# A hybrid decoder layer on one core: the last attention pair ahead of two gate blocks, weight differences at a fixed place, results picked up one unit later

## The chip, the cores and the metric

The kernel runs on one core of a Trainium2 chip. The metric is device time in microseconds for one call. TensorE (PE) multiplies matrices, VectorE (DVE) and ScalarE (ACT) do the elementwise work, GpSimd (POOL) issues some transfers, and SyncE (SP) issues the weight loads. Each engine works through its own instructions in order.

## The reference

Input x is 256 tokens of 2048 channels, all in float32. A pre-norm is followed by one wide input projection and two token mixers: a gated delta rule over 8 heads (short convolution, decays, a triangular inverse in chunks of 64), and causal attention over 8 heads of 128. With 256 tokens there is one attention block, so no past block is ever chosen. Both results are gated, widened to 2048 channels, merged and projected once more:

```python
proj = h @ w_in                      # q, k, v, z of both mixers, gate_a, gate_b
u_a = oa @ w_branch_a                # 256 x 1024 by 1024 x 2048
u_b = (ob * silu(moba_z)) @ w_branch_b
merged = sigmoid(gate_a) * u_a + sigmoid(gate_b) * u_b
x = x + rms_norm(merged @ w_out, post_norm_w)
```

## The kernel before, in words

**Split weights.** Every weight tile is loaded in float32 by SP (`raw`, 1 MB, three buffers) and split into a rounded half `hi`, cast by ACT (L218), and a rest `lo`, subtracted by DVE (L219), each with three buffers. A product is then three matmuls (hi by hi, lo by hi, hi by lo) into PSUM, which has 4 `acc` banks for projections and 4 `aux` banks for all smaller work. One split of 128 x 1024 elements feeds 12 matmuls of 512 columns in a gate block, or 16 mixed ones in a query or key block. That is one **unit** of the kernel's clockwork below.

**Blocks and ORDER.** The string `ORDER` (L42) is the sequence of blocks on PE. `q`, `kq`, `v` are the delta rule's projections, `zg` and `zm` the two output gates, `mv` attention's values, and `mk0` to `mk3` attention's queries and keys of two heads each. `ga0` to `ga3` and `gb0` to `gb3` are blocks of 512 columns of the two merging gates (`sigmoid_gate`, L708). `ua0` and `ua1` are pairs of 512-column blocks of `oa @ w_branch_a`. After ORDER come the four blocks of branch b (`branch`, L1036, "ub"), with their merging, and the output projection (`y`).

**Seven products for a pair.** A pair (`seven`, L766) is a 2 x 2 block product done with seven products in place of eight. It needs sums of quarters of the activations (`oas`, made by `turned_outputs`, L913) and differences of quarters of the weights (`tq`, three tiles fetched by POOL at L724 and subtracted by DVE in six operations at L731). Between its products it takes `fill` work: the four row blocks of one gate, before the change ga2 for the first pair and ga3 for the second. `done` (L804) multiplies a finished quarter, c11, c12, c22 or c21, into the gate. The first pair's differences are asked for inside `solve`; `next_differences` (L818) asks for those of the second pair and then for those of the output projection.

**Queues.** Everything that isn't a projection stands in queues of Python generators. While a projection is written down, `tick()` (L136) runs after every half unit and lets each queue go on when its wait is over. A generator says with `yield n` how many units it waits. `gq` holds the delta rule (`decays`, `score_pair`, `inverse`, `solve`), `vq` its values, `aq` two queues of attention heads (`attend`, L979), `bq` the turning of attended heads, `mq` the merging, and `sq` the differences (`differences`, L726, which first waits T_WAIT). So a wait in units says beside which projection work an instruction is written down. While `turned_outputs` runs, `held` stops `aq` and `bq`, because it keeps all four `aux` banks.

**attend** writes the scores after A_WAIT1 = 1.5 units, the transposes of the softmaxed scores A_WAIT2 later, and the product with the values A_WAIT3 later. Its two heads run side by side in two queues.

**What fixes the order on an engine.** The order of writing is a wish: an instruction whose inputs are expected early can be moved ahead of earlier ones on its engine. `pin` holds an instruction behind the one written just before it on the same engine. All PE work is pinned. Of DVE's work a part is, not the differences at L731.

Of the kernel before, what the change touches and what calls it, by code (L numbers as in the profile page):

```python
# [8 lines left out]
F32 = mybir.dt.float32  # L9
F32R = mybir.dt.float32r  # L10
BF16 = mybir.dt.bfloat16
AF = mybir.ActivationFunctionType
ALU = mybir.AluOpType
AX = mybir.AxisListType

P = 128
# [11 lines left out]
LC_WAIT = (1.5, 1.5, 1.5, 3.5)  # L28
INV = (0.6, 2)
SLOW = 8  # L30
T_WAIT = 3
V_WAIT = 8
SV_WAIT = 1
OS_WAIT = 3
A_WAIT1 = 1.5
A_WAIT2 = 6
A_WAIT3 = 3
A_WAIT4 = 4

ORDER = (  # L42
    "q0 mv0 zg0 q1 kq2 kq3 zg1 v0 v1 v2 ga0 zm0 zm1 mv1 v3 mk0 mk1 mk2 ga1 mk3 ua0 gb0 gb1 ua1 gb2 gb3"
).split()


# [28 lines left out]
def hybrid_layer(  # L75
# [15 lines left out]
    nc = tc.nc  # L91
    B, S, D = x.shape
    NT = S // P
    KT = D // P
    H = a_log.shape[1]
# [6 lines left out]
    w_in = w_in.rearrange("o d f -> (o d) f")  # L102
# [6 lines left out]
    CGA = CMQ + 4 * GW  # L109
    CGB = CGA + D  # L110

    cst = ctx.enter_context(tc.tile_pool(name="cst", bufs=1))
    big = ctx.enter_context(tc.tile_pool(name="big", bufs=1))
    wraw = ctx.enter_context(tc.tile_pool(name="wraw", bufs=3))
    wspl = ctx.enter_context(tc.tile_pool(name="wspl", bufs=3))
    wk = ctx.enter_context(tc.tile_pool(name="wk", bufs=2))
# [7 lines left out]
    def aux_tile(name):  # L124
        return aux.tile([P, 512], F32, tag="aux", name=name)
# [6 lines left out]
    extra = []  # L132
# [418 lines left out]
    def lazily(make):  # L551
        made = []

        def get():
            if not made:
                made.append(make())
            return made[0]

        return get
# [125 lines left out]
        v_left[0] -= 1  # L685
        after[0] = SLOW

    ga012 = big.tile([P, D // 512 - 1, NT, 512], F32, tag="ga", name="ga")

    ga3 = lazily(lambda: big.tile([P, NT, 512], F32, tag="ga3", name="ga_3"))  # L690

    def ga(c, t):
        return ga012[:, c, t, :] if c < 3 else ga3()[:, t, :]


    def free_tile(shape, dtype, tag, name):
        gq.drain()
# [5 lines left out]
    def ob_tile():  # L703
        while not obs:
            gq.tick()
        return obs[0]

    def sigmoid_gate(n, col, c):  # L708
        pts = proj_n(w_in, col + c * 512, hT, KT, f"{n}{c}")
        for t in range(NT):  # L710
            tl = ga(c, t) if n == "ga" else gb_tile()[:, c, t, :]
            nc.scalar.activation(tl, pts[t], AF.Sigmoid, scale=rstd[:, t : t + 1])

    oaT = [None]

# [10 lines left out]
    def differences(tq, c, wait):  # L726
        yield wait
        for o, a, b in ((0, 0, 2), (1, 1, 0), (2, 1, 2)):
            for u in range(2):
                us = slice(2 * u, 2 * u + 2)  # L730
                nc.vector.tensor_tensor(tq[o][:, us], tq[a][:, us], tq[b][:, us], op=ALU.subtract)  # L731
                yield 1
        formed.append(c)

# [27 lines left out]
    def load(w, h, c, name):  # L762
        raw = wraw.tile([P, 4, 512], F32, tag="raw", name=f"raw_{name}{c}_{h}")
        nc.sync.dma_start(raw, w[h * 512 : (h + 1) * 512, c * 512 : (c + 1) * 512].rearrange("(k p) c -> p k c", p=P))
        return raw

    def seven(quarter, s_, tq, w, c, banks, name, fill=lambda i: None, done=lambda b: None):
        c11, c12, c21, c22 = banks
        s5 = tq[0][:, 0]
        product([quarter(0, 0)], load(w, 0, c, name), [c21], [True], f"{name}p1")  # L770
        fill(0)
        product([s_[0]], tq[0], [c12], [True], f"{name}p5")
        nc.scalar.copy(c11, c21)
        product([s_[1]], tq[1], [c21], [False], f"{name}p6")
        nc.scalar.copy(s5, c12)
        fill(1)
        raw21 = load(w, 1, c, name)
        nc.vector.tensor_tensor(c12, c21, s5, op=ALU.add)
        product([quarter(0, 1)], raw21, [c11], [False], f"{name}p2")
        for u in range(2):  # L780
            us = slice(2 * u, 2 * u + 2)
            nc.vector.tensor_tensor(tq[1][:, us], raw21[:, us], tq[1][:, us], op=ALU.subtract)  # L782
        product([s_[2]], tq[2], [c21], [False], f"{name}p7")
        fill(2)
        nc.vector.tensor_tensor(c22, c21, s5, op=ALU.add)
        done(c11)
        product([s_[3]], load(w, 1, c + 1, name), [c12], [False], f"{name}p3")
        fill(3)
        done(c12)
        done(c22)  # L790
        product([quarter(1, 1)], tq[1], [c21], [False], f"{name}p4")
        done(c21)

    def branch_pair(i):
        c = 2 * i
        while not oas or c not in formed:
            sq.tick()
            gq.tick()
        c11, c12, c21, c22 = (acc_tile(f"a_ua{c}_{n}") for n in ("11", "12", "21", "22"))
        place = {id(c11): (c, 0), id(c12): (c + 1, 0), id(c21): (c, 1), id(c22): (c + 1, 1)}  # L800

        def done(b):
            cc, t = place[id(b)]
            nc.vector.tensor_tensor(ga(cc, t), ga(cc, t), b, op=ALU.mult)  # L804


        quarter = quarters(hT)
        pts = [aux_tile(f"a_ga{2 + i}_{t}") for t in range(NT)]

        def gate(h):  # L810
            raw = load(w_in[:, CGA : CGA + D], h, 2 + i, "ga")
            product([quarter(0, h), quarter(1, h)], raw, pts, [h == 0] * 2, f"ga{2 + i}_{h}")
            if h == 3:
                for t in range(NT):
                    nc.scalar.activation(ga(2 + i, t), pts[t], AF.Sigmoid, scale=rstd[:, t : t + 1])

        seven(quarters(oaT[0]), oas, tqs[-1], wa, c, (c11, c12, c21, c22), f"ua{c}", fill=gate, done=done)

    def next_differences(w, c):

        for q in aq + bq:
            q.drain()
        tqs.append([big.tile([P, 4, 512], F32, tag=f"z{i}", name=f"tq{len(tqs)}_{i}") for i in range(3)])
        for i in (0, 2, 1):
            fetch(tqs[-1], w, c, i)
        formed.clear()
        sq.add(differences(tqs[-1], c, T_WAIT))

    def solve():
# [83 lines left out]
        def turned_outputs(ozs):  # L913


            a = {}
            for t in (1, 0):
                for g in range(2):
                    pt = aux_tile(f"ot_{t}_{g}")
                    for hh in range(4):  # L920
                        tr(pt[:, hh * P : (hh + 1) * P], ozs[t][:, g, hh, :], ident)
                    a[t, g] = pt.rearrange("p (h n) -> p h n", n=P)
                for g in range(2):
                    ks = slice(4 * g, 4 * g + 4)
                    halved(oT[:, ks, t * P : (t + 1) * P], oT[:, ks, S + t * P : S + (t + 1) * P], a[t, g])
                yield 1
            oa_f = big.tile([P, 2, 4, P], F32, tag="tv", name="oa_f")
            x, y = (oa_f[:, i] for i in range(2))
            nc.scalar.copy(x, a[1, 1])
            nc.vector.tensor_tensor(a[1, 1], a[1, 0], x, op=ALU.add)  # L930
            nc.scalar.copy(y, a[0, 0])
            nc.vector.tensor_tensor(a[0, 0], a[1, 1], y, op=ALU.subtract)
            nc.scalar.copy(x, a[0, 0])
            yield 0.5
            nc.vector.tensor_tensor(a[0, 1], a[0, 1], x, op=ALU.subtract)
            nc.vector.tensor_tensor(a[1, 0], y, a[1, 0], op=ALU.subtract)
            yield 0.5
            sums = [None] * 4
            for i, o, tag in ((0, (1, 1), "tt"), (1, (0, 0), "tw"), (3, (0, 1), "ga3"), (2, (1, 0), "tv")):
                tl = big.tile([P, 2, 4, P], F32R, tag=tag, name=f"oas_{i}")  # L940
                sums[i] = tl[:, 0], tl[:, 1]
                halved(*sums[i], a[o])
                yield 0.5
            oas.extend(sums)
# [19 lines left out]
            fetch(tqs[0], wa, 0, i)  # L964
        sq.add(differences(tqs[0], 0, T_WAIT))
        yield OS_WAIT
        held.append(True)
        yield from turned_outputs(ozs)
        held.pop()
# [3 lines left out]
    def attention_values(c):  # L973
        pts = proj_n(w_in, CMV + c * 512, hT, KT, f"mv{c}")
        for t in range(NT):
            nc.scalar.activation(mv[:, t, c * 512 : (c + 1) * 512], pts[t], AF.Copy, scale=rstd[:, t : t + 1])


    def attend(h, qT, kT):  # L979
        yield A_WAIT1  # L980
# [16 lines left out]
            tr(pp[:, b * P : (b + 1) * P], s[:, b * P : (b + 1) * P], ident)  # L997
        pT = wk.tile([P, 3 * P], F32, tag="pT", name=f"pT_{h}")
        nc.scalar.copy(pT, pp[:, : 3 * P])
        yield A_WAIT3  # L1000
        po = aux_tile(f"po_{h}")
        hc = slice(h * P, (h + 1) * P)
# [31 lines left out]

    def branch(c):
        pb = proj_n(wb, c * 512, ob_tile(), H, f"ub{c}")  # L1036
        for t in range(NT):
            nc.vector.tensor_tensor(gb_tile()[:, c, t, :], gb_tile()[:, c, t, :], pb[t], op=ALU.mult)  # L1038
        for t in range(NT):
            nc.vector.tensor_tensor(ga(c, t), ga(c, t), gb_tile()[:, c, t, :], op=ALU.add)  # L1040

    for m in range(4):
        kTs[m // 2].append(halves(pfirst[m], f"k{m}"))
# [65 lines left out]

    for c in range(D // 512):  # L1110
        branch(c)
        mq.add(merge(c, 0.5 if c < 3 else 5))


    quarter = quarters(mT)
# [54 lines left out]
    c = 3  # L1170
    pts = [acc_tile(f"a_y{c}_{t}") for t in range(NT)]
    keep = []
    for tg, n in (("g0", 4), ("ga", 3), ("ga3", 1), ("u1", 4)):
        tl = big.tile([P, n, 2, 512], F32R, tag=tg, name=f"keep_{tg}")
        keep += [tl[:, i] for i in range(n)]
    parts = []
# [53 lines left out]
```

## Time and profile before

| | |
|---|---|
| median of 3 runs | 792.16 us (789.65 to 792.6) |
| profiled execution | 790.07 us, span 788.4 us |
| mean granted clock of TensorE | 0.994 |
| matmuls | 3923 |
| memory read, written | 149.61 MB, 3.15 MB |

A row of a timeline gives the start and the duration in us, the engine, the line, what is written from what, the count of merged instructions, and in brackets the idle time of the engine before it and what ended that. A row of the windows gives for a stretch the busy time and count of each engine, then the granted clock as a share of full speed, the busy share of the DMA engines and GB/s. The profile's names leave out buffer numbers: `a_mq` is the PSUM bank of an attention query projection, `a_ga` of a gate block, `tq` a tile of weight quarters. In the trace mk2 lies at 363 to 402.5 us, ga1 at 402.5 to 434.5, mk3 at 434.5 to 465.4, the first pair at 465.4 to 513.7, gb0 and gb1 at 513.7 to 559.2, the second pair at 559.2 to 602.6, gb2 and gb3 at 602.6 to 646.5, branch b at 646.5 to 694.3, and the output projection after it.

### The profile page before, as it was taken

To read this page: it belongs to the slowest core of one execution; us is meant where nothing else is said; L and a number is where in the kernel's file an instruction comes from. 1 tells how busy PE (TensorE), PEld (TensorE's weight loads), DVE (VectorE), ACT (ScalarE), POOL (GpSimd) and SP (SyncE) were. 2 spreads that over 40 slices of the span, in tenths; PEclk is the share of its full clock that TensorE was granted. 3 is DMA by queue.
4 is the path that set the end of the run, shared out by engine and by line. 5 is a ranking of instruction groups with operands and counts; after the bars stand their busy time and mean duration, and the time that the engine had idled before them with its cause. 6 is when DMAs were issued, how large, how long until landed. Compare 5 with 4: busy or idle time off the path is not lost. (4 is left out here: it accounts for less than half of the span.)

```text
span 788.4 us, 10325 instructions
## 1 busy us (share of the span) xinstructions
PE 767.4 (97%) x3923; PEld 651.6 (83%) x3923; DVE 565.0 (72%) x914; ACT 425.3 (54%) x642; POOL 29.0 (4%) x53
## 2 busy tenths in 40 slices
PE   8999999999999999999999899999999999999996
PEld 7998988898888888888888688878877888787884
DVE  5777679886768898774556968784588546878573
ACT  5676665656544444454454756634554444556551
POOL 3000000102000000011001000100000000000000
PEclk9999999999999999999999899999999999999999
DMA  8485766459864656659337362766467564584542
GB/s 306 162 259 187 206 187 170 141 178 227 263 209 163 211 170 205 183 165 241 101 114 266 105 204 83 280 234 203 173 224 270 200 211 163 163 315 170 208 158 106
DMA packets 93399, 153.42 MB, mean 195 GB/s; under 512 B 3109, under 2 KB 46758, under 8 KB 92710
## 3 DMA queue, kind: packets, MB, share of 16 engines
q1 hardware_dynamic: 88902, 134.42, 52.7%
q0 software_dynamic: 3872, 17.31, 6.9%
q10 hardware_dynamic: 576, 1.05, 0.4%
q8 instruction: 30, 0.49, 0.3%
q14 instruction: 19, 0.16, 0.1%
HBM read 149.61 MB, written 3.15 MB: 194 GB/s over the span
## 5 line engine op out<-in xcount | busy, mean ns | idle before, releaser
L144 PE MATMUL a_ga<-hi_ga,hT 128*128 128x512 f32 x256 | 84.1, 396 | 0.0
L144 PE MATMUL a_gb<-hi_gb,hT 128*128 128x512 f32 x256 | 79.2, 389 | 0.0
L219 DVE TENSOR_TENSOR lo_gb<-raw_gb,hi_gb 128x1024 fp32r<-128x1024 f32 x32 | 38.9, 1222 | 26.6 <-ACT hi_gb L218 26.6
L144 PEld LDWEIGHTS a_gb<-hi_gb,hT 128*128 128x128 f32 x256 | 48.1, 188 | 9.9
L144 PEld LDWEIGHTS a_ga<-hi_ga,hT 128*128 128x128 f32 x256 | 48.1, 188 | 9.6
L218 ACT CAST hi_gb<-raw_gb 128x1024 fp32r<-128x1024 f32 x32 | 33.4, 1053 | 41.3 <-PE a_gb L144 37.5
L219 DVE TENSOR_TENSOR lo_ga<-raw_ga,hi_ga 128x1024 fp32r<-128x1024 f32 x32 | 38.8, 1222 | 23.5 <-ACT hi_ga L218 23.3
L144 PE MATMUL a_ga<-lo_ga,hT 128*128 128x512 f32 x128 | 50.4, 394 | 2.2 <-DVE lo_ga L219 2.2
L144 PE MATMUL a_gb<-lo_gb,hT 128*128 128x512 f32 x128 | 50.1, 391 | 1.7 <-DVE lo_gb L219 1.7
L144 PE MATMUL a_mq<-hT,hi_mq 128*128 128x512 f32 x128 | 48.7, 419 | 2.8 <-ACT hi_mq L218 2.8
L218 ACT CAST hi_ga<-raw_ga 128x1024 fp32r<-128x1024 f32 x32 | 33.4, 1052 | 25.6 <-PE a_ga L144 13.5
L144 PE MATMUL a_zg<-hi_zg,hT 128*128 128x348 f32 (+1 forms) x192 | 47.0, 322 | 0.0
L144 PE MATMUL a_mk<-hT,hi_mk 128*128 128x512 f32 x128 | 46.4, 404 | 0.0
L144 PE MATMUL a_y<-hi_y,mT 128*128 128x512 f32 x144 | 45.9, 391 | 0.0
L144 PE MATMUL a_q<-hT,hi_q 128*128 128x512 f32 x128 | 45.8, 398 | 0.0
L144 PE MATMUL a_v<-hT,hi_v 128*128 128x512 f32 x128 | 45.5, 399 | 0.1
L144 PE MATMUL a_ub<-hi_ub,obT 128*128 128x512 f32 x128 | 41.2, 394 | 0.0
L144 PE MATMUL a_k<-hT,hi_k 128*128 128x512 f32 x128 | 40.4, 398 | 0.5 <-ACT hi_k L271 0.5
L144 PE MATMUL a_zm<-hi_zm,hT 128*128 128x512 f32 x128 | 40.6, 392 | 0.0
L144 PE MATMUL a_mv<-hi_mv,hT 128*128 128x512 f32 x128 | 40.1, 390 | 0.0
L144 PE MATMUL a_mq<-hT,lo_mq 128*128 128x256 f32 x128 | 37.1, 290 | 1.1 <-DVE lo_mq L219 1.1
L144 PE MATMUL a_v<-hT,lo_v 128*128 128x256 f32 x128 | 36.0, 282 | 0.8 <-DVE lo_v L219 0.8
(362 smaller groups left out, 1958.6 us busy)
## 6 DMA issues: line engine op xcount, KB each, us to landing
raw_ga<-in_w_in_dram SPq DMA_DIRECT2D x16, 1024.0 KB, 5.2
raw_gb<-in_w_in_dram SPq DMA_DIRECT2D x16, 1024.0 KB, 5.1
raw_y<-in_w_out_dram SPq DMA_DIRECT2D x15, 1024.0 KB, 5.0
raw_q<-in_w_in_dram SPq DMA_DIRECT2D x8, 1024.0 KB, 5.6
raw_mv<-in_w_in_dram SPq DMA_DIRECT2D x8, 1024.0 KB, 5.1
raw_v<-in_w_in_dram SPq DMA_DIRECT2D x8, 1024.0 KB, 5.7
raw_zm<-in_w_in_dram SPq DMA_DIRECT2D x8, 1024.0 KB, 5.3
raw_mq<-in_w_in_dram SPq DMA_DIRECT2D x8, 1024.0 KB, 5.7
```

Source lines behind the costliest of these rows:

```text
L144: return pin(nc.tensor.matmul(*args, **kwargs))
L218: nc.scalar.copy(hi, raw)
L219: nc.vector.tensor_tensor(lo, raw, hi.bitcast(F32), op=ALU.subtract)
```

## The change

Six edits, with no change to what is computed:

1. ORDER: mk3 follows mk2 directly; ga1 and ga2 are blocks ahead of the first pair; ga3 is the first pair's filling and gb2 the second's.
2. Waits: A_WAIT2 6 to 4, A_WAIT3 3 to 2, T_WAIT 3 to 7, and the first three merges wait 1.5 units where they waited 0.5.
3. The differences at L731 are pinned, and `next_differences` asks for its three tiles in another order.
4. `turned_outputs` waits until all eight heads have their softmax transposed; the sums for the product p3 lie in two softmax buffers ("s") in place of a tile of their own.
5. The gate of branch a is one tile of four blocks in place of three and one.
6. c21's multiplication, and branch b's multiplications and additions, go into a new queue `dq` and are written down one unit later.

```diff
-T_WAIT = 3
+T_WAIT = 7
...
-A_WAIT2 = 6
-A_WAIT3 = 3
+A_WAIT2 = 4
+A_WAIT3 = 2
...
-    "q0 mv0 zg0 q1 kq2 kq3 zg1 v0 v1 v2 ga0 zm0 zm1 mv1 v3 mk0 mk1 mk2 ga1 mk3 ua0 gb0 gb1 ua1 gb2 gb3"
+    "q0 mv0 zg0 q1 kq2 kq3 zg1 v0 v1 v2 ga0 zm0 zm1 mv1 v3 mk0 mk1 mk2 mk3 ga1 ga2 ua0 gb0 gb1 ua1 gb3"
...
-    ga012 = big.tile([P, D // 512 - 1, NT, 512], F32, tag="ga", name="ga")
-    ga3 = lazily(lambda: big.tile([P, NT, 512], F32, tag="ga3", name="ga_3"))
+    ga_ = big.tile([P, D // 512, NT, 512], F32, tag="ga", name="ga")
...
-                nc.vector.tensor_tensor(tq[o][:, us], tq[a][:, us], tq[b][:, us], op=ALU.subtract)
+                pin(nc.vector.tensor_tensor(tq[o][:, us], tq[a][:, us], tq[b][:, us], op=ALU.subtract))
...
-        done(c21)
+        dq.add(later(lambda: done(c21)))
+
+    dq = Queue()
+    extra.append(dq)
+
+    def later(f):
+        yield 1
+        f()
...
+        n, g, col = (("ga", 3, CGA), ("gb", 2, CGB))[i]
+        pts = [aux_tile(f"a_{n}{g}_{t}") for t in range(NT)]
...
-        for i in (0, 2, 1):
+        for i in (2, 0, 1) if len(tqs) == 2 else (1, 0, 2):
             fetch(tqs[-1], w, c, i)
...
+                    sums[i] = [wk.tile([P, 4, P], F32R, tag="s", name=f"oas_{i}_{n}") for n in ("hi", "lo")]
...
         yield OS_WAIT
+        while attended[0] < H:
+            yield 0.5
         held.append(True)
         yield from turned_outputs(ozs)
...
+        attended[0] += 1
         yield A_WAIT3
...
+        def weighted():
+            for t in range(NT):
+                nc.vector.tensor_tensor(gb_tile()[:, c, t, :], gb_tile()[:, c, t, :], pb[t], op=ALU.mult)
+            for t in range(NT):
+                nc.vector.tensor_tensor(ga(c, t), ga(c, t), gb_tile()[:, c, t, :], op=ALU.add)
+
+        dq.add(later(weighted))
...
-        mq.add(merge(c, 0.5 if c < 3 else 5))
+        mq.add(merge(c, 1.5 if c < 3 else 5))
...
-    for tg, n in (("g0", 4), ("ga", 3), ("ga3", 1), ("u1", 4)):
+    for tg, n in (("g0", 4), ("ga", 4), ("u1", 4)):
```

More of the change, by code (lines that the diff above doesn't have):

```diff
@@ L686, in values @@
         after[0] = SLOW
-    ga012 = big.tile([P, D // 512 - 1, NT, 512], F32, tag="ga", name="ga")
-    ga3 = lazily(lambda: big.tile([P, NT, 512], F32, tag="ga3", name="ga_3"))
+    ga_ = big.tile([P, D // 512, NT, 512], F32, tag="ga", name="ga")
     def ga(c, t):
-        return ga012[:, c, t, :] if c < 3 else ga3()[:, t, :]
+        return ga_[:, c, t, :]
     def free_tile(shape, dtype, tag, name):
@@ L706, in ob_tile, with gate_place @@
         return obs[0]
+    def gate_place(n, c, t):
+        return ga(c, t) if n == "ga" else gb_tile()[:, c, t, :]
     def sigmoid_gate(n, col, c):
@@ L710, in sigmoid_gate @@
         for t in range(NT):
-            tl = ga(c, t) if n == "ga" else gb_tile()[:, c, t, :]
-            nc.scalar.activation(tl, pts[t], AF.Sigmoid, scale=rstd[:, t : t + 1])
+            nc.scalar.activation(gate_place(n, c, t), pts[t], AF.Sigmoid, scale=rstd[:, t : t + 1])
     oaT = [None]
@@ L807, in branch_pair @@
         quarter = quarters(hT)
-        pts = [aux_tile(f"a_ga{2 + i}_{t}") for t in range(NT)]
+        n, g, col = (("ga", 3, CGA), ("gb", 2, CGB))[i]
+        pts = [aux_tile(f"a_{n}{g}_{t}") for t in range(NT)]
         def gate(h):
-            raw = load(w_in[:, CGA : CGA + D], h, 2 + i, "ga")
-            product([quarter(0, h), quarter(1, h)], raw, pts, [h == 0] * 2, f"ga{2 + i}_{h}")
+            raw = load(w_in[:, col : col + D], h, g, n)
+            product([quarter(0, h), quarter(1, h)], raw, pts, [h == 0] * 2, f"{n}{g}_{h}")
             if h == 3:
                 for t in range(NT):
-                    nc.scalar.activation(ga(2 + i, t), pts[t], AF.Sigmoid, scale=rstd[:, t : t + 1])
+                    nc.scalar.activation(gate_place(n, g, t), pts[t], AF.Sigmoid, scale=rstd[:, t : t + 1])
         seven(quarters(oaT[0]), oas, tqs[-1], wa, c, (c11, c12, c21, c22), f"ua{c}", fill=gate, done=done)
@@ L938, in turned_outputs @@
             sums = [None] * 4
-            for i, o, tag in ((0, (1, 1), "tt"), (1, (0, 0), "tw"), (3, (0, 1), "ga3"), (2, (1, 0), "tv")):
-                tl = big.tile([P, 2, 4, P], F32R, tag=tag, name=f"oas_{i}")
-                sums[i] = tl[:, 0], tl[:, 1]
+            for i, o, tag in ((0, (1, 1), "tt"), (1, (0, 0), "tw"), (3, (0, 1), None), (2, (1, 0), "tv")):
+                if tag:
+                    tl = big.tile([P, 2, 4, P], F32R, tag=tag, name=f"oas_{i}")
+                    sums[i] = tl[:, 0], tl[:, 1]
+                else:
+                    sums[i] = [wk.tile([P, 4, P], F32R, tag="s", name=f"oas_{i}_{n}") for n in ("hi", "lo")]
                 halved(*sums[i], a[o])
@@ L976, in attention_values @@
             nc.scalar.activation(mv[:, t, c * 512 : (c + 1) * 512], pts[t], AF.Copy, scale=rstd[:, t : t + 1])
+    attended = [0]
     def attend(h, qT, kT):
@@ L1036, in branch @@
         pb = proj_n(wb, c * 512, ob_tile(), H, f"ub{c}")
[L1037 to L1040, printed above, removed]
+        def weighted():
[4 more added lines that the diff above has]
+        dq.add(later(weighted))
     for m in range(4):
```

## The prediction

> **What bounds the kernel now.** The page comes first: engines, then the granted clock by slice.
>
> ```profile
> PE 767.4 (97%) x3923; PEld 651.6 (83%) x3923; DVE 565.0 (72%) x914; ACT 425.3 (54%) x642; POOL 29.0 (4%) x53
> ...
> PEclk9999999999999999999999899999999999999999
> ```
>
> PE (TensorE) is busy nearly throughout, and no matmul is added or removed. What can change is the time in which PE stands still, and the one slice in which its clock was not granted in full. So the second view is the waits of PE, longest first (total, times, longest).
>
> ```profile
> PE a_mq L144 <- ACT hi_mq L218: 2.8, 1, 2.8
> PE a_ga L144 <- DVE lo_ga L219: 2.2, 3, 1.1
> PE a_gb L144 <- DVE lo_gb L219: 1.7, 1, 1.7
> ...
> PE a_mq L144 <- DVE lo_mq L219: 1.1, 1, 1.1
> ...
> PE a_ub L144 <- DVE lo_ub L219: 0.5, 1, 0.5
> ...
> PE a_y L144 <- DVE lo_y L219: 0.4, 1, 0.4
> PE mt L147 <- DVE ga L1040: 0.2, 1, 0.2
> ```
>
> Every long one is a wait for the hi or lo half of a weight, so ACT (ScalarE) and DVE (VectorE) fell behind there. Third, the windows of the three stretches around the longest: gate block ga1 with the delta rule's closing work, the queries half of mk3, its keys half (columns: PE, PEld, DVE, ACT, POOL busy with counts, clock, DMA).
>
> ```profile
> 402.57:434.53 31.96, 31.96 (x184) 27.66 (x182) 20.33 (x45) 17.75 (x53) 2.28 (x3) 1.00 0.65 220
> 434.53:453.64 19.11, 15.17 (x74) 12.62 (x72) 17.36 (x24) 14.75 (x25) 0.00 (x0) 0.82 0.34 110
> 453.64:465.40 11.76, 11.76 (x69) 10.15 (x68) 7.49 (x11) 5.26 (x8) 0.00 (x0) 1.00 0.54 180
> ```
>
> The two halves of mk3 hold the same 64 weight matmuls, yet the queries take 19.11 us and the keys 11.76, and only in the first is the clock below 1. The timelines of DVE and ACT say why.
>
> ```profile
> 428.79 2.36 DVE L731 TENSOR_TENSOR tq_g<-tq_g 128x1024 f32<-128x1024 f32 x2 [2.94 <-DMA tq_g<-in_w_branch_a_dram]
> 431.07 1.22 DVE L219 TENSOR_TENSOR lo_mq<-raw_mq,hi_mq 128x1024 fp32r<-128x1024 f32 x1
> 432.20 0.35 DVE L987 SCALAR_TENSOR_TENSOR s<-ms,qscale,mask_m 128x128 f32<-128x128 f32 x1
> ...
> 434.22 0.41 DVE L990 TENSOR_REDUCE mx<-s 128x1 f32<-128x256 f32 x1
> 434.55 1.21 DVE L731 TENSOR_TENSOR tq_z<-tq_z,tq_g 128x1024 f32<-128x1024 f32 x1
> ...
> 438.26 2.35 DVE L731 TENSOR_TENSOR tq_g<-tq_z,tq_g 128x1024 f32<-128x1024 f32 x2
> ```
>
> ```profile
> 440.08 1.06 ACT L218 CAST hi_mq<-raw_mq 128x1024 fp32r<-128x1024 f32 x1
> ```
>
> DVE stands 2.94 us on a difference whose weights have not landed, then does six differences, two heads' softmax preparation and the turned outputs in one run. ACT waits for DVE's maxima, and the next hi_mq is cast only at 440.08. Four things that are each cheap fell into 12 us.
>
> **The change part by part.** I count in units: one split of 1024 columns feeds 12 matmuls, and the splits of an undisturbed gate block lie one unit, 552.38 - 549.66 = 2.72 us, apart.
>
> ```profile
> 549.66 1.22 DVE L219 TENSOR_TENSOR lo_gb<-raw_gb,hi_gb 128x1024 fp32r<-128x1024 f32 x1 [1.49 <-ACT hi_gb L218]
> 552.38 1.22 DVE L219 TENSOR_TENSOR lo_gb<-raw_gb,hi_gb 128x1024 fp32r<-128x1024 f32 x1 [1.50 <-ACT hi_gb L218]
> ```
>
> *The new order, A_WAIT2 and A_WAIT3, and the wait for all eight heads.* Let mk2 end at unit 16. Before, a head pair holds its queue for 1.5 + 6 + 3 = 10.5 units although a pair is added every 8, so the scores of heads 4 and 5 slip to 22.5, beside the differences and the turned outputs (23.5). After, a pair takes 7.5 units and keeps pace. mk3 fills 16 to 24 with the delta rule's norms (16.5 to 20.5) and the scores of heads 4, 5 (17.5). ga1 fills 24 to 32 with the scores of heads 6, 7 (25.5), their transposes (29.5), the differences (27 to 32) and, from 30, the turned outputs, which end near 35 inside ga2. The first branch pair starts at 40, so the added wait for eight heads blocks nothing: behind it in its queue stands only the turning itself, needed 5 units later. The crowd at 434.53 goes: 19.11 - 11.76, less about 0.5 for four more transposes, is **6.85 us**. The 2.81 and 1.12 us waits are its idle part, and the rest is the halved clock: 0.18 x 19.11 = 3.4 us, partly under the second wait.
>
> ```profile
> 441.19 0.80 PE L144 MATMUL a_mq<-hT,hi_mq 128*128 128x512 f32 x1 [2.81 <-ACT hi_mq L218]
> ...
> 443.11 0.58 PE L144 MATMUL a_mq<-hT,lo_mq 128*128 128x256 f32 x1 [1.12 <-DVE lo_mq L219]
> ...
> 486.71 0.50 PE L144 MATMUL a_ga<-lo_ga,hT 128*128 128x512 f32 x1 [0.65 <-DVE lo_ga L219]
> ...
> 515.78 0.50 PE L144 MATMUL a_gb<-lo_gb,hT 128*128 128x512 f32 x1 [1.69 <-DVE lo_gb L219]
> ...
> 597.26 0.50 PE L144 MATMUL a_ga<-lo_ga,hT 128*128 128x512 f32 x1 [1.15 <-DVE lo_ga L219]
> ```
>
> The scores of heads 6, 7 leave the first pair as well, and with them the wait of **0.65** at 486.71.
>
> The Trainium skill, "TensorE: Matmul & The Clock Gate", Part 1, says that the clock falls to half after an idle window of about 3.4 us that runs freely. The trace agrees loosely: 2.81 us of idle were enough, 1.69 and 1.15 were not. By that rule a new wait of the longest kind costs its halved clock again, as the rows did.
>
> *Results a unit later (c21, and the gate products of branch b).* After the first pair DVE waits for PE's last product with three splits queued behind it:
>
> ```profile
> 513.91 0.69 DVE L804 TENSOR_TENSOR ga<-ga,a_ua 128x512 f32<-128x512 f32 x1 [3.15 <-PE a_ua L144]
> 514.51 3.49 DVE L219 TENSOR_TENSOR lo_gb<-raw_gb,hi_gb 128x1024 fp32r<-128x1024 f32 x3
> ```
>
> With the product due a unit later the splits go first, and PE's **1.69** goes; ACT's table load at the same place goes too, since no exponential is left in the pair. In branch b four products stand ahead of a split: 0.47 (the a_ub row) and 0.2 (mt) go, **0.67**. The bank of c21 is held a unit longer; the gate block behind it has the banks of c11 and c12, so that costs nothing unless those are late too.
>
> *T_WAIT 7, differences held.* The pair-2 stall has the same form as the first:
>
> ```profile
> 594.84 1.23 DVE L731 TENSOR_TENSOR tq<-tq,tq 128x1024 f32<-128x1024 f32 x1 [2.04 <-DMA tq<-in_w_out_dram]
> 595.99 1.22 DVE L219 TENSOR_TENSOR lo_ga<-raw_ga,hi_ga 128x1024 fp32r<-128x1024 f32 x1
> ```
>
> Seven units are 19 us after the fetches are asked for; DVE runs at most three splits ahead (three buffers), so 11 us remain. The median landing times are 5.4 to 10.6 us.
>
> ```profile
> tq<-in_w_out_dram POOLq DMA_DIRECT2D x3, 1024.0 KB, 5.4
> ...
> tq_z<-in_w_branch_a_dram POOLq DMA_DIRECT2D x1, 1024.0 KB, 10.6
> ```
>
> So **1.15** goes. What the six differences (7.3 us) meet in their new place: for pair 2, a bare gate block; for w_out, the last unit of gb3 and then branch b.
>
> ```profile
> 650.00:660.00 10.00, 9.88 (x47) 7.92 (x46) 6.53 (x8) 3.92 (x5) 0.00 (x0) 1.00 0.51 172
> 660.00:670.00 10.00, 10.00 (x48) 8.27 (x47) 6.20 (x8) 5.12 (x8) 0.00 (x0) 1.00 0.46 161
> 670.00:680.00 10.00, 9.83 (x48) 7.90 (x47) 9.07 (x14) 6.29 (x9) 0.00 (x0) 1.00 0.64 210
> ```
>
> DVE has 3.5 and 3.8 us free per 10 us there, and the products that used to close ub0 move out of it, so about five differences (6.1 us) just fit before the crowd at 670. Bounds 0 and 6.1 us; I take 0.5.
>
> *Moved DMA and PSUM.* SP's loads of mk3 come ahead of those of ga1 and ga2, same sizes. POOL's three fetches for the first pair now meet mk3's rest and ga1's loads; three buffers of 5.4 us each cover those. I take 0; at worst it is a wait like DVE's on landing, 2.94 us. The fetches' order (2, 0, 1 and 1, 0, 2) is 0, as each tile comes free only when its last reader is done. One gate tile in place of two, and sums in the softmax buffers, which eight attended heads have left: 0. ga2, ga3 and gb2 change places as block or filling, with the same matmuls.
>
> *What is new in mk3.* Its norms now meet queries, keys and softmax. Two groups of DVE, the norms' products and the joining of a projection's two halves (busy, mean ns, idle):
>
> ```profile
> L897 DVE SCALAR_TENSOR_TENSOR oz<-so,fo,zg 128x128 f32<-128x128 f32 x16 | 4.3, 342 | 0.1
> ...
> L455 DVE TENSOR_TENSOR y_mk<-a_mk,y_mk 128x256 f32<-128x256 f32 x8 | 3.3, 418 | 0.0
> ```
> The nearest row is the first window: there the same norms, a pair's scores and transposes, and two differences left DVE busy 20.33 and ACT 17.75 of 31.96 us without a PE wait. mk3 swaps the differences (-2.4) for the joining of its halves (six operations of 0.42 us, 2.5 in all) and one table load. DVE stays under 70%. Locally, from 16.5 to 20.5, the norms, two heads' scores (2.4 us) and the splits come close to PE's time, with two splits of lead. The same closeness holds around 30 to 34 in ga1 and ga2. Bounds: 0, and once more the whole 6.85. I take 1.0, nearest to the first window.
>
> The Trainium skill, "ScalarE: Activation LUTs", "What ACT_TABLE_LOAD costs", gives about 2.66 us for each switch, drain included. The trace's row is less:
>
> ```profile
> 480.16 1.28 ACT L991 ACT_TABLE_LOAD   x1
> 481.45 0.40 ACT L991 ACTIVATE s<-s,mx 128x128 f32<-128x128 f32 x1
> ```
>
> By that page mk3's extra switch would take 1.4 us more of ACT, which is idle for more than that.
>
> *The sum.* Gone: 6.85 + 0.65 + 1.69 + 0.67 + 1.15 = 11.0, and about 0.4 for the slow first matmul (0.50 for 0.39 us) behind each wait. New: 0.5 + 1.0. Net -9.9 us. The profiled execution took 790.07 us (span 788.4), so 780.2; the three runs lie from 789.65 to 792.6, median 792.16. A new median may lie as far above its profile, so I add about half of that 2.1: **781.3 us**.
>
> **The rivals.**
>
> *The crowd moves into mk3 or ga1 once* (norms or turned outputs meeting heads and differences). For it: four in-order sources within 4 units. Against: no PE wait in the first window. Time: one more cluster in place of the 1.5 allowed, -4.1 to -4.6, 786 to 788; with 3 us from the fetches, 790.5.
>
> *The differences are not where they are meant to be* (the edit does not do what it says): DVE still meets unlanded weights. Then 1.15 and perhaps 1.69 stay, and one 2.94 wait sits in ga1 under two splits of lead: 784 to 787.
>
> *Slower.* Place: mk3. DVE's queue is in order, and norms, halves and scores (4.3 + 2.5 + 2.4 = 9.2 us besides the splits) can stand ahead of lo halves while ACT fetches a square root's and an exponential's table (2 x 1.28). If the lead is gone when they come, PE stands for all of it, in two pieces (one for each half of the sequence), each long enough to halve the clock at another 3.4 us: 9.2 + 2.6 + 6.8 = 18.6 us against 11.4 gained, 797 to 799. It decides from the point where more than 11.4 us are uncovered. Against: the same norms cost PE nothing in the first window.
>
> **How the numbers follow.** Forecast 0.62 (own range 777 to 785); the crowd moved 0.16; differences not held 0.11; slower 0.11. The range 777 to 790.5 takes in the first three: its low end is all 11.4 us gained with nothing new, 778.7, and the two small waits left in the seven-product steps. It leaves out the slower case and little more. Half a per cent, 4 us, is about what a measurement of this kernel can tell from no change: faster is below 788.2. That gives faster 0.76 (part of the moved crowd lies above), same 0.12, slower 0.12.
>
> **What would show it.** Right: the clock row is 9 throughout after the head; no PE wait over 1 us after the v blocks; no DVE wait on tq's DMA ahead of a lo; the lo_gb splits ahead of the last ga product. Wrong: a PE wait near 3 us in mk3, ga1 or ga2 with the clock below 1; DVE idle on tq; DVE full in branch b with a_ub waiting.

## The result and the profile after

The kernel after takes 783.03 us (median of 4 runs, 782.47 to 784.34), the kernel before beside it 791.98 (4 runs, 789.65 to 792.6): a ratio of 0.9895, 95% interval 0.9871 to 0.9919. That is faster by 9 us by the medians and 8.3 by the ratio, 1.7 above the forecast of 781.3 and inside its range. The profiled execution took 782.64 us (span 780.9, mean clock 0.998), 7.43 less than that of before, where the sum had promised 9.9.

The page of the kernel after, its engines and its clock row:

```profile
PE 765.3 (98%) x3923; PEld 651.5 (83%) x3923; DVE 565.3 (72%) x914; ACT 425.2 (54%) x642; POOL 29.0 (4%) x53
...
PEclk9999999999999999999999999999999999999999
```

The slice with an 8 is gone: every slice is granted 90% or more, and the mean clock rose from 0.994 to 0.998. PE is busy 2.1 us less with the same 3923 matmuls. The waits of PE after (total, times, longest):

```profile
PE a_ga L144 <- DVE lo_ga L219: 1.9, 2, 1.6
PE a_ub L144 <- DVE lo_ub L219: 1.5, 1, 1.5
...
PE a_gb L144 <- DVE lo_gb L219: 0.4, 1, 0.4
```

The waits of a_mq, 2.8 and 1.1, are gone, and so is a_gb's 1.7: the 0.4 in this list stands in the second pair's filling, which is now gb2 and had the same 0.37 us as ga3. Two waits of about 1.5 us are left, and a_ub's has grown from 0.5.

Where the 7.43 us came from is read from two long windows, from the gate block ga0 to the start of branch b and from there to the last output matmul. Before, then after (columns as in the prediction: length, then the busy time of PE and the others, clock ahead of the DMA share):

```profile
215.70:646.47 430.77, 422.92 (x2113) 354.07 (x2112) 305.42 (x463) 221.28 (x313) 12.09 (x17) 0.99 0.59 191
646.47:780.38 133.91, 132.77 (x597) 108.44 (x595) 92.93 (x105) 68.85 (x86) 1.26 (x2) 1.00 0.54 189
```

```profile
216.49:638.62 422.13, 419.66 (x2113) 352.11 (x2112) 302.63 (x462) 221.30 (x313) 12.09 (x17) 1.00 0.60 195
638.62:772.95 134.33, 132.40 (x597) 108.62 (x595) 96.20 (x108) 68.85 (x86) 1.26 (x2) 1.00 0.54 188
```

The matmuls are the same, 2113 and 597. The first stretch is 8.64 us shorter: PE's busy time fell by 422.92 - 419.66 = 3.26 (above all, matmuls no longer run at a lowered clock), its idle time from 7.85 to 2.47, by 5.38. The second stretch is 0.42 longer. The first block starts 216.49 - 215.70 = 0.79 later, which arises in the head, where every engine has the same instructions in the same order; in the traces of all the kernels here this block starts between 215.45 and 218.22. -8.64 + 0.42 + 0.79 = -7.43.

The two places where the crowd could have reappeared are mk3, and ga1 with ga2. Windows of the kernel after:

```profile
405.09:436.65 31.56, 31.56 (x208) 28.56 (x207) 20.83 (x50) 21.66 (x61) 2.28 (x3) 1.00 0.60 212
436.65:488.20 51.55, 49.99 (x244) 41.59 (x243) 39.16 (x54) 31.04 (x47) 0.75 (x1) 1.00 0.54 182
```

mk3 shows PE busy for all of its 31.56 us, DVE busy for 20.83 (66%), and the clock at 1.00. ga1 and ga2 lose 1.56 us, all of it in one wait, in ga2 (timeline of PE, kernel after):

```profile
470.57 0.51 PE L144 MATMUL a_ga<-lo_ga,hT 128*128 128x512 f32 x1 [1.56 <-DVE lo_ga L219]
```

DVE's timeline ahead of it, after:

```profile
463.32 1.22 DVE L730 TENSOR_TENSOR tq_g<-tq_z,tq_g 128x1024 f32<-128x1024 f32 x1
...
467.98 1.40 DVE L920 SCALAR_TENSOR_TENSOR oas<-ot,pcol,oas 128x512 fp32r<-128x512 f32 x2
469.30 1.22 DVE L219 TENSOR_TENSOR lo_ga<-raw_ga,hi_ga 128x1024 fp32r<-128x1024 f32 x1
```

From 463.32 to 469.30 DVE works without a pause, but on two differences (L730) and the turned outputs (L920 to L945) alone, and no lo is made. ACT in the same time, with a table load and, between the two rows, sigmoids and copies ahead of the next cast:

```profile
462.48 1.28 ACT L711 ACT_TABLE_LOAD   x1
...
465.41 1.05 ACT L218 CAST hi_ga<-raw_ga 128x1024 fp32r<-128x1024 f32 x1
```

Which of these makes the wait is left to the experiments. The other wait stands in branch b. DVE there, after:

```profile
670.29 0.68 DVE L1120 TENSOR_TENSOR sums_f<-mt,sums_f 128x512 f32<-128x512 f32 x1
...
674.09 1.28 DVE L1057 TENSOR_TENSOR gb<-gb,a_ub 128x512 f32<-128x512 f32 x2
...
676.49 1.22 DVE L219 TENSOR_TENSOR lo_ub<-raw_ub,hi_ub 128x1024 fp32r<-128x1024 f32 x1
```

The merging's sums (L1120 to L1128) run first, and right behind them the two multiplications and two additions that the change writes a unit later (the "four products"); together 6.2 us without a lo. The window around it, after:

```profile
670.00:680.00 10.00, 8.54 (x38) 6.75 (x37) 9.97 (x16) 5.23 (x7) 0.00 (x0) 1.00 0.19 60
```

DVE is busy for 9.97 of the 10 us.

Last, the first gate block after the first pair, where 1.69 us were lost before. DVE after:

```profile
529.87 1.23 DVE L219 TENSOR_TENSOR lo_gb<-raw_gb,hi_gb 128x1024 fp32r<-128x1024 f32 x1 [2.06 <-ACT hi_gb L218]
531.01 0.68 DVE L811 TENSOR_TENSOR ga<-ga,a_ua 128x512 f32<-128x512 f32 x1
```

The split goes ahead of c21's product, as the prediction said. But ACT differs at this place too. Before:

```profile
509.51 1.28 ACT L815 ACT_TABLE_LOAD   x1
...
511.96 2.99 ACT L218 CAST hi_gb<-raw_gb 128x1024 fp32r<-128x1024 f32 x3
```

After, there is no table load here: the sigmoids start at 527.53 and the casts at 528.79. Two edits can claim the 1.69.

### The profile page after: what moved, and what is told of

It reads as the page before. It is cut to its first block, busy times and chain, and to the rows that moved or that the text cites. A ratio compares the mean times of both kernels' runs of the same rounds, so it can differ in the third digit from the quotient of the medians.

```text
span 780.9 us, 10336 instructions
## 1 busy us (share of the span) xinstructions
PE 765.3 (98%) x3923; PEld 651.5 (83%) x3923; DVE 565.3 (72%) x914; ACT 425.2 (54%) x642; POOL 29.0 (4%) x53
## 3 DMA queue, kind: packets, MB, share of 16 engines
HBM read 149.61 MB, written 3.15 MB: 196 GB/s over the span
## 4 chain that ended last, share of the span: by engine, by line
PE 88%; DVE 5%; DMA 3%; ACT 2%; issue 1%; DVEq 0%; SPq 0%; ACTq 0%
PE a_gb L144 11%; PE a_y L144 10%; PE a_ga L144 10%; PE a_zg L144 6%; PE a_mq L144 6%; PE a_mk L144 6%; PE a_k L144 6%; PE a_zm L144 6%; PE a_mv L144 5%; PE a_ub L144 5%; PE a_q L144 4%; PE a_v L144 4%; PE a_ua L144 3%; DMA raw_v<-in_w_in_dram 2%; PE sv L144 2%; PE s L144 1%
## 5 line engine op out<-in xcount | busy, mean ns | idle before, releaser
L144 PE MATMUL a_ga<-hi_ga,hT 128*128 128x512 f32 x256 | 82.0, 394 | 0.0
L144 PE MATMUL a_mq<-hT,hi_mq 128*128 128x512 f32 x128 | 46.9, 407 | 0.0
L144 PE MATMUL a_mk<-hT,lo_mk 128*128 128x256 f32 x128 | 35.9, 281 | 0.0
```

The source lines that it names most:

```text
L144: return pin(nc.tensor.matmul(*args, **kwargs))
```

## The experiments

The theory at this point: the crowd at mk3's queries was many short DVE and ACT jobs within 12 us, and all of it went because heads, norms, differences and turned outputs now lie apart. The rivals: that one part of the change does it alone, and that the gains at the pair and in branch b were credited to the wrong edits. Each kernel's time stands beside runs of the kernel before on the same chip (medians: 791.54 us for the four on the order, the differences held or loose, and the heads' waits undone; 790.98 for c21 or branch b's products at once, the sums later and the differences late; 791.15 for the rest). Each edit is against the kernel named.

**mk3 ahead of ga1, in the kernel before.** All else stays: ga2 is still the first pair's filling, so this is one part of the new order and not the whole of it.

```diff
- mk2 ga1 mk3 ua0
+ mk2 mk3 ga1 ua0
```

> The kernel before with one edit: mk3 stands ahead of ga1 (ga2, ga3 and gb2 stay where they were, all waits and the loose differences stay). Theory (crowding): six differences, two heads' softmax preparation and the turned outputs still fall into one stretch of some 12 us, now beside ga1's splits; PE waits about 4 us there, the clock halves again, and the time is 789 to 793. Rival (the order itself does it, since mk3's queries were what was late): the cluster of 6.85 us goes, 784 to 786.

Measured: 789.94 us, ratio 0.9978 [0.9964, 0.9992]. PE's waits in its ga1, one after the other:

```profile
440.27 0.50 PE L144 MATMUL a_ga<-lo_ga,hT 128*128 128x512 f32 x1 [1.38 <-DVE lo_ga L219]
444.51 0.50 PE L144 MATMUL a_ga<-lo_ga,hT 128*128 128x512 f32 x1 [1.19 <-DVE lo_ga L219]
449.08 0.50 PE L144 MATMUL a_ga<-lo_ga,hT 128*128 128x512 f32 x1 [1.55 <-DVE lo_ga L219]
```

The crowd moved into ga1 and broke into four waits (the fourth is 0.57). The time is the theory's, its halved clock isn't: the granted clock stayed at 1.00 around all four. This part of the order alone is worth 1.6 us.

**The differences held, in the kernel before.**

```diff
-T_WAIT = 3
+T_WAIT = 7
...
-                nc.vector.tensor_tensor(tq[o][:, us], tq[a][:, us], tq[b][:, us], op=ALU.subtract)
+                pin(nc.vector.tensor_tensor(tq[o][:, us], tq[a][:, us], tq[b][:, us], op=ALU.subtract))
```

> The kernel before with the differences pinned and T_WAIT 7, nothing else. Theory (crowding): DVE no longer stands on unlanded weights and the differences spread over mk3, so the wait in mk3's queries falls from 3.9 us to under 1.5 and its halved clock goes (5 to 6 us), and the 1.15 in the second pair goes: 784 to 787. Rival (the order and the heads' waits made the gain): only the 1.15 goes, 789 to 791.

Measured: 787.37 us, ratio 0.9935 [0.9916, 0.9954]. The longest of its waits in mk3:

```profile
448.66 0.39 PE L144 MATMUL a_mq<-hT,lo_mq 128*128 128x256 f32 x1 [1.14 <-DVE lo_mq L219]
```

There are three more, of 0.52, 0.77 and 0.83, and with about 0.1 us for the slow first matmul behind each the four cost some 3.7 us; but the clock stays at 1.00, and pair 2's 1.15 is gone; gb0's 1.7 stays. The time lies just above the expected 784 to 787. So the unlanded weights were one part of the crowd, not the whole: without them the jobs still crowd, in smaller pieces.

**The heads' waits alone, in the kernel before.**

```diff
-A_WAIT2 = 6
-A_WAIT3 = 3
+A_WAIT2 = 4
+A_WAIT3 = 2
```

> The kernel before with the heads' new waits alone (A_WAIT2 4, A_WAIT3 2). The scores of heads 4 and 5 then lie 6 units ahead of the turned outputs, the loose differences and the turned outputs still together on unlanded weights. Theory (crowding): one of four sources leaves the crowd, the waits at mk3's queries fall from 3.9 us to 1.5 to 3 and the clock stays: 785.5 to 788.5. Rival (DVE's stand on the weights' landing rules the cluster): the cluster stays whole, 790 to 792.

Measured: 792.21 us, ratio 1.0011 [0.9998, 1.0024]: no gain, and the theory's number was wrong. PE and then DVE, in this kernel:

```profile
441.58 1.17 PE L147 MATMUL ot<-ident,oz 128*128 128x128 f32 x8 [3.15 <-DVE zm L1009]
...
456.10 0.39 PE L144 MATMUL a_mk<-hT,lo_mk 128*128 128x256 f32 x1 [1.82 <-DVE lo_mk L219]
```

```profile
431.91 2.36 DVE L731 TENSOR_TENSOR tq_g<-tq_g 128x1024 f32<-128x1024 f32 x2 [3.66 <-DMA tq_g<-in_w_branch_a_dram]
```

DVE stands 3.66 us on the unlanded difference with everything queued behind it. The heads that come sooner only change who waits at the end of it: now the turned outputs, for an aux bank still held by a head's output.

**The heads' waits undone, in the kernel after.**

```diff
-A_WAIT2 = 4
-A_WAIT3 = 2
+A_WAIT2 = 6
+A_WAIT3 = 3
```

> The changed kernel with the old waits of the heads (A_WAIT2 6, A_WAIT3 3). The last heads are then attended at unit 39 where 40 begins the first pair, so the turned outputs (8.4 us of DVE) are written down in one piece ahead of it. Theory (crowding): PE waits 3 to 6 us at the start of the first pair, perhaps with the clock halved: 785 to 791. Rival (the heads' waits are of no account, the order gives room enough): 782 to 784.

Measured: 790.37 us, ratio 0.9973 [0.9957, 0.9989]: most of the gain is lost, 6.2 us by the ratios (0.9973 against 0.9895). The waits of its PE, and the window around the first of them:

```profile
PE a_ga L144 <- DVE oas L920: 3.1, 1, 3.1
PE a_ua L144 <- ACT oaT L919: 1.8, 1, 1.8
```

```profile
487.00:493.00 6.00, 4.24 (x11) 3.08 (x12) 4.26 (x7) 5.24 (x8) 0.00 (x0) 0.72 0.28 107
```

The turned outputs now wait for the eighth head, and the pair that needs them has begun: the mean clock is 0.72 here, and 0.66 from 493 to 502 around the longer wait. The profiled execution took 792.54 us, the longest of twelve that begin at 787.46, and has the lowest mean clock of them (0.988), so it shows more of the lowered clock than most. An edit worth nothing by itself carries the new order.

**The differences loose, in the kernel after.** T_WAIT back to 3 and the pin taken off L730.

```diff
-T_WAIT = 7
+T_WAIT = 3
...
-                pin(nc.vector.tensor_tensor(tq[o][:, us], tq[a][:, us], tq[b][:, us], op=ALU.subtract))
+                nc.vector.tensor_tensor(tq[o][:, us], tq[a][:, us], tq[b][:, us], op=ALU.subtract)
```

> The changed kernel with the differences loose again and T_WAIT 3. Theory (crowding): the 1.15 wait in the second pair returns and DVE stands some 3 us on the first pair's weights in mk3, but the turned outputs come 6 units later, so no cluster; the 1.56 wait in ga2 goes, since differences no longer lie among the turned outputs: 782 to 785, clock 1. Rival (held differences are the gain): the cluster returns, 788 to 791.

Measured: 785.09 us, ratio 0.9909 [0.9889, 0.993], against 0.9895 with them held: 1.1 us by the ratios, whose intervals overlap. The trace is clearer: DVE stands 4.0 us on tq_g's transfer, a wait of 1.1 us in ga1 (ms, for y_mk) and one of 1.3 in pair 2 are new, and ga2's falls from 1.56 to 0.55. The hold is worth 1 to 2 us here, less than the 4.2 in the kernel before, where the unlanded weights stood in the crowd.

**c21's product at once, in the kernel after.**

```diff
-        dq.add(later(lambda: done(c21)))
+        done(c21)
```

> The changed kernel with c21 multiplied at once, as before, in both pairs. The prediction's step: DVE waits again for PE's last product with the gate block's splits behind it, PE's 1.69 us returns after the first pair and some 0.2 after the second: 784.5 to 785. Rival: the splits stood behind c21 only because an exponential's table load in the first pair made hi_gb late; with no exponential there the splits go first anyhow, and nothing changes: 783.0 within 0.7, with no wait over 0.3 us at the first gate block.

Measured: 782.12 us, ratio 0.9888 [0.9871, 0.9904], and every wait behind the head is that of the kernel after. On every engine the instructions stand in the same order as there: the edit does nothing.

**c21 a unit later, in the kernel before.** The same queue as in the change, for c21 alone.

> The kernel before with c21 multiplied one unit later in both pairs, nothing else. The prediction's step: the 1.69 us wait at the first gate block after the first pair goes, 789.5. Rival (the order there is set by the table load, not by where c21 is written): the 1.69 stays and the time is that of the kernel before, 790.5 to 792.

Measured: 791.46 us, ratio 1.0008 [0.9996, 1.002]. Its DVE:

```profile
514.20 0.69 DVE L811 TENSOR_TENSOR ga<-ga,a_ua 128x512 f32<-128x512 f32 x1 [3.15 <-PE a_ua L144]
514.80 3.49 DVE L219 TENSOR_TENSOR lo_gb<-raw_gb,hi_gb 128x1024 fp32r<-128x1024 f32 x3
```

Written a unit later, the product still stands ahead of the splits, and a_gb still waits 1.7 us; here too every engine's order is that of the kernel without the edit.

**A table load brought forward, in the kernel before.** One sigmoid of one column is added on ACT in the pair's third filling; nothing uses its result.

```diff
+            if h == 2 and i == 0:
+                tl = wk.tile([P, 1], F32, tag="rstd", name="early")
+                pin(nc.scalar.activation(tl, epst, AF.Sigmoid))
```

> The kernel before with one sigmoid of one column added on ACT in the first pair's third filling, so that the sigmoid table is loaded a filling earlier than the gate's own sigmoids; its result is used by nothing. Theory (table load makes hi_gb late): the wait at the first gate block falls from 1.69 us to under 0.4: 789 to 790.5. Rival (c21's wait for PE is the cause): it stays 1.69.

Measured: 789.29 us, ratio 0.9977 [0.9967, 0.9987]. ACT and then DVE, in this kernel:

```profile
510.83 1.37 ACT L818 ACTIVATE ga<-a_ga,rstd 128x512 f32<-128x512 f32 x2 [1.01 <-PE a_ga L144]
512.10 3.19 ACT L218 CAST hi_gb<-raw_gb 128x1024 fp32r<-128x1024 f32 x3
```

```profile
513.17 1.22 DVE L219 TENSOR_TENSOR lo_gb<-raw_gb,hi_gb 128x1024 fp32r<-128x1024 f32 x1 [2.09 <-ACT hi_gb L218]
514.31 0.68 DVE L804 TENSOR_TENSOR ga<-ga,a_ua 128x512 f32<-128x512 f32 x1
```

The table load is gone from this place, and the first split now stands ahead of the product; PE's a_gb wait is gone from the list. The casts run at nearly the time they had before (512.10 for 511.96), so it is the order on DVE that counts, and taking the table load away from here turned that order round. That the expected times of instructions do this when the order is laid down is likely, but not shown. Pair 2's wait is 0.81 here for 1.15, which is in the gain as well.

**Branch b's products at once, in the kernel after.**

```diff
-        dq.add(later(weighted))
+        weighted()
...
-        mq.add(merge(c, 1.5 if c < 3 else 5))
+        mq.add(merge(c, 0.5 if c < 3 else 5))
```

> The changed kernel with branch b's products written down at once and the merges' wait 0.5, as before. Theory (crowding): the 1.46 us wait in branch b comes of the later products, which meet the four sums of the merge; at once, they take the old places, the wait falls to the 0.47 and 0.2 of before: 782. Rival: the 1.46 comes of the differences for w_out, which now reach into branch b; it stays or grows: 783 to 784.5.

Measured: 782.48 us, ratio 0.9892 [0.9875, 0.9908]. The wait of its PE for a split of branch b:

```profile
PE a_ub L144 <- DVE lo_ub L219: 0.5, 1, 0.5
```

That is the 0.5 of the kernel before, mt's 0.2 is back as well, and the last stretch takes the 133.91 us that it took before. The differences for w_out are in this kernel too, so by themselves they do not make the wait of 1.46. The times can't tell the two kernels apart; the traces can.

**The sums two units later, in the kernel after.** What moves is the splitting of the merging's sums (L1127, L1128).

```diff
             for i, j in enumerate((2, 3, 1, 0)):
-                yield 1
+                yield 1 if i else 3
```

> The changed kernel with the four sums of the merge written down two units later (all else equal, summed still ahead of the product that reads them). Theory (crowding in branch b by sums and products): the 1.46 us wait falls to under 0.5, 781.5 to 782.5. Rival (differences, or DVE full throughout branch b): it stays or moves, 783 to 784.

Measured: 781.81 us, ratio 0.9885 [0.987, 0.9899]. a_ub and a_y are no longer in the list of waits. The last stretch, and DVE where sums and products had run as one:

```profile
640.26:772.46 132.20, 132.12 (x597) 108.67 (x595) 95.99 (x108) 68.75 (x86) 1.26 (x2) 1.00 0.54 191
```

```profile
673.85 1.22 DVE L219 TENSOR_TENSOR lo_ub<-raw_ub,hi_ub 128x1024 fp32r<-128x1024 f32 x1
...
675.59 1.27 DVE L1057 TENSOR_TENSOR gb<-gb,a_ub 128x512 f32<-128x512 f32 x2
```

A split now lies ahead of the products, and the stretch takes 132.20 us for 134.33 after and 133.91 before. The time alone, 0.9885 for 0.9895, would not show it. So the later products did harm only because the sums were due at the same place; whether they are worth anything themselves isn't shown, as later sums with products at once were not run.

**The first pair's differences 7.5 units later, in the kernel after.**

```diff
-        sq.add(differences(tqs[0], 0, T_WAIT))
+        sq.add(differences(tqs[0], 0, 14.5))
```

> The changed kernel with the first pair's differences 7.5 units later (wait 14.5 in place of 7), behind the turned outputs. Theory (crowding): of the DVE work ahead of the late split in ga2 two or three differences of 1.2 us go, its wait of 1.56 falls to under 0.6: 781.5 to 782.5. Rival: ACT is what is late there (a table load, two sigmoids and the halves of the turned outputs); the wait stays over 1.2: 783.

Measured: 783.23 us, ratio 0.9902 [0.9887, 0.9917]. The wait in ga2, and DVE ahead of it:

```profile
473.85 0.50 PE L144 MATMUL a_ga<-lo_ga,hT 128*128 128x512 f32 x1 [1.67 <-DVE lo_ga L219]
```

```profile
470.78 0.74 DVE L920 SCALAR_TENSOR_TENSOR oas<-ot,pcol,oas 128x512 fp32r<-128x512 f32 x1
471.44 1.21 DVE L730 TENSOR_TENSOR tq_g<-tq_g 128x1024 f32<-128x1024 f32 x1
472.57 1.22 DVE L219 TENSOR_TENSOR lo_ga<-raw_ga,hi_ga 128x1024 fp32r<-128x1024 f32 x1
```

The wait did not shrink, but the place was not cleared either: the first difference now stands between the last of the turned outputs and the late split. The kernel with the differences loose, above, is the cleaner test. There all six are done before, and the split comes right behind the last of the turned outputs:

```profile
471.64 1.22 DVE L219 TENSOR_TENSOR lo_ga<-raw_ga,hi_ga 128x1024 fp32r<-128x1024 f32 x1
```

```profile
472.91 0.50 PE L144 MATMUL a_ga<-lo_ga,hT 128*128 128x512 f32 x1 [0.55 <-DVE lo_ga L219]
```

So without the differences 0.55 us are left, with the turned outputs where they were. One difference ahead of the split adds the 472.57 - 471.44 = 1.13 by which it delays it, 1.68 in all for the measured 1.67. It takes both to make the wait. ACT is not what this split waited for: its hi half had been cast by 469.50.

**The turned outputs spread, and the sums later, in the kernel after.** Three waits inside the turning go from half a unit to one, beside the edit of the sums above.

```diff
-            yield 0.5
+            yield 1
...
-                yield 1
+                yield 1 if i else 3
```

> The changed kernel with the sums of the merge two units later, as in the run that moved them alone, and the steps of the turned outputs one unit apart in place of half a unit. Theory (crowding on ACT and DVE by the turned outputs themselves): the 1.56 us wait in ga2 falls to under 0.5 beside the gain in branch b: 780 to 781.5, the fastest of all. Rival: the turned outputs now reach the first pair, where the attention outputs held back by them fall too, and PE waits there: 782 or more.

Measured: 779.97 us (4 runs, 779.33 to 780.82), ratio 0.9863 [0.9846, 0.9881], the fastest of all the kernels here. Its DVE in ga2, and PE's wait:

```profile
467.69 0.74 DVE L920 SCALAR_TENSOR_TENSOR oas<-ot,pcol,oas 128x512 fp32r<-128x512 f32 x1
468.35 1.21 DVE L219 TENSOR_TENSOR lo_ga<-raw_ga,hi_ga 128x1024 fp32r<-128x1024 f32 x1
469.48 0.74 DVE L920 SCALAR_TENSOR_TENSOR oas<-ot,pcol,oas 128x512 fp32r<-128x512 f32 x1
```

```profile
469.61 0.50 PE L144 MATMUL a_ga<-lo_ga,hT 128*128 128x512 f32 x1 [0.89 <-DVE lo_ga L219]
```

The turned outputs' last steps (L920) and the splits now alternate, and the lo that PE waits for is made at 468.35 in place of 469.30. The median lies just below the 780 to 781.5 that was expected; the wait, expected under 0.5, is still 0.89.

## Why the prediction was right, point by point

*The crowd at mk3's queries (6.85), the heads' 0.65 and pair 2's 1.15: right.* PE lost 3.26 us of slow matmuls and 5.38 us of idle time in the stretch that holds them. mk3 has no wait, so neither the moved crowd nor the slower case came about there. The experiments add what the prediction could not say: none of the parts tried does it alone. mk3 ahead of ga1 -1.6, differences held -4.2, heads' waits +1.1, c21 +0.3 (medians, each against the kernel before on its chip) make -4.4, while the whole change makes -9.0. The heads' waits, worth nothing alone, are worth about 6 us inside. ga2 as a block of its own, the wait for eight heads, the fetches' order and, in the kernel before, branch b's later products were not tried alone, so how much of the rest is theirs and how much is interplay stays open.

*The stretch from ga0 to branch b.* Forecast: 6.85 + 0.65 + 1.69 + 1.15 + 0.4 - 1.0 = 9.74 less. Measured: 8.64 less. Nearly all of the missing 1.1 is idle time, and the term that was sized too small is the one for what is new, taken as 1.0: ga2's wait is 1.56 us, and one of 0.37 in the first pair's filling is new too. The place, the turned outputs around 30 to 34, had been named. The forecast had not worked out what the runs show there: 0.55 us where the turned outputs stand without the differences, and about 1.1 more for a difference put ahead of the late split.

*c21 (1.69): the amount right, the edit wrong, so partly luck.* The step said that the product, due a unit later, would let the splits go first. The splits do go first after, but whether the product is written at once or later makes no difference in either kernel. What had to go was ACT's table load, which the prediction named in half a sentence as going too. It goes because the last exponentials have left the first pair.

*Branch b (0.67 gone, 0.5 new): the step that failed.* The a_ub wait was to go and grew from 0.47 to 1.46 instead, since the products moved back by one unit run into the sums of the merging. The price was put on the wrong suspect: the w_out differences cost nothing (with the products at once the stretch takes 133.91 us as before, differences and all). The prediction had quoted the row of the crowd at 670 to 680, DVE 9.07 of 10 us, and had not asked whether the four moved products end up in it. Forecast for the last stretch -0.17, measured +0.42.

*The remaining 0.79* of the shortfall from 9.9 to 7.43 lies in the head, where no edit changes the order: 1.10 + 0.59 + 0.79 = 2.48. The added 1.1 for the median was 0.4 (783.03 - 782.64).

*What would show it.* The clock row, the splits ahead of the last ga product, and DVE's waits (none on tq's transfers is left) are as said. "No PE wait over 1 us after the v blocks" is false: there are two, 1.56 and 1.46. Of the signs of being wrong one came: DVE full in branch b, 9.97 of 10 us, with a_ub waiting.

## What to carry to other kernels

When a job is moved by a unit, write down what is already due at the new place: here the waits were not any one job but several cheap ones that fell between two splits, and an edit worth nothing alone carried others. Before crediting a gain to an edit, look for everything else that differs at that place, and undo the edit alone; then look in the trace whether the undoing really cleared the place. On an in-order engine a small delay upstream (here a 1.28 us table load on ACT) can cost through the order in which the next engine's work is put down, not through its own length.

## What the runs showed of the hardware

The clock fell after shorter idle times than the 2.81 us for which the prediction had a row. In the kernel before with the heads sooner, two windows at PE's waits of 3.15 and 1.82 us (the 6 us between them show 1.00):

```profile
442.00:448.00 6.00, 6.00 (x30) 5.16 (x28) 6.00 (x9) 3.37 (x5) 0.00 (x0) 0.72 0.22 76
...
454.00:460.00 6.00, 4.17 (x16) 3.36 (x15) 3.87 (x5) 1.32 (x2) 0.00 (x0) 0.72 0.29 77
```

The first window follows the 3.15 us wait, the last holds the one of 1.82, and both show a mean clock of 0.72. In the kernel before the crowd's two waits show that the lowered clock is the half:

```profile
441.00:446.00 5.00, 3.69 (x10) 2.79 (x11) 5.00 (x8) 4.05 (x7) 0.00 (x0) 0.51 0.35 89
446.00:451.00 5.00, 5.00 (x26) 4.31 (x25) 4.37 (x6) 3.07 (x6) 0.00 (x0) 0.80 0.46 139
```

At half, a mean of 0.72 over 6 us is 2 x 0.28 x 6 = 3.4 us of lowered clock, and these two rows are 2 x (0.49 + 0.20) x 5 = 6.9, twice that. The same 0.72 stands in the kernel before with c21 later, over 596 to 602 us, at a wait of 1.92, and above at the 1.8 us wait of the kernel after with its heads' waits undone. Waits of 1.69 (gb0, in the kernel before and in its variants with mk3 ahead, differences held, heads sooner and c21 later), 1.67 (ga2, with the differences late), 1.56 and 1.46 (after) did not lower it. The Trainium skill, "TensorE: Matmul & The Clock Gate", Part 1, speaks of an idle window of about 3.4 us; here 1.82 us of idle time were enough. What decides between 1.69 and 1.82 isn't shown: it may be the length, or where the wait falls in a window that runs freely.
